# Spreading a group norm's factor over all partitions: two matmuls with a diagonal, or a round trip through DRAM on GpSimd's queue

## The chip, the cores and the metric

The kernel runs on one core of a Trainium2 chip. The metric is the device time of one execution in microseconds; the time before is the median of three runs. The profile is of one further execution. TensorE (PE) does matmuls, VectorE (DVE) and ScalarE (ACT) work on tiles in SBUF and PSUM, GpSimd (POOL) does small copies and products, and SyncE (SP) issues every transfer of the kernel before.

## The reference, cut to what matters

One step of a hybrid decoder layer. A prompt of 256 tokens with 16 learned tokens ahead of it, and 8 sample sequences of 8 tokens, go through an input projection, a Mamba-2 scan (64 heads in 8 groups), a short gated convolution, a merge of the two, and an output projection. The change touches the norm behind the scan:

```python
def gated_group_rms_norm(y, z, w):
    g = y.astype(jnp.float32) * jax.nn.silu(z.astype(jnp.float32))
    shp = g.shape
    g = g.reshape(shp[:-1] + (SSD_GROUPS, shp[-1] // SSD_GROUPS))
    g = g * lax.rsqrt(jnp.mean(g * g, axis=-1, keepdims=True) + EPS)
    return (g.reshape(shp) * w.astype(jnp.float32)).astype(y.dtype)
```

For each token and each of the 8 groups one factor, the inverse root of a mean over 512 channels, multiplies these 512 channels. All is float32; the kernel gets this accuracy by splitting each matmul operand into a rounded part and a rest (`hi`, `lo`).

## The kernel before, in words

All 336 tokens (320 are wanted in the end, `TV`) lie on the free axis and channels on the partitions. A weight tile of 128 outputs comes in two blocks of 128x1024 (`wblk`, L82 to L89): SP loads `wraw` (L84), ACT rounds it to `whi` (L86), DVE makes the rest `wlo` (L88). Each of the three tiles has three buffers. For each block TensorE multiplies eight pieces of `whi` with the rounded input and with its rest (L94, L95), then eight pieces of `wlo` with the rounded input (L98). So the `wlo` that DVE makes is read 16 matmuls after its `whi`. A projection unit (`unit`, `proj`) is two such blocks into one PSUM tile `pj`, of which there are two.

The scan is the function `ssd(g, st)`, a generator with `yield` between its steps, run for g = 0 to 7. `weave` (L677) runs the steps of `ssd(g)` between the projection units of the same stage: the gates `z_units(g)`, the output projection of the group before `out_units(g - 1)` (its inputs are `yh` and `yl`), and the convolution inputs of the next group `conv_units(g + 1)`; stage 7 has gate units in place of the last. Steps are spread evenly by matmul work. A scheduler then sets the order on each engine by times that it reckons for every instruction; each engine and SP's queue work in that fixed order.

At the end of `ssd(g)`:

- L602: three matmuls with a column of ones sum the squares, 107 tokens on partitions and 3 columns (321 = 320 tokens and a zero).
- L604 (DVE) scales and adds EPS, L605 (POOL) takes the power -0.5: `rs_r`, 107x3.
- L607 and L608 (DVE) split it into `rs_h`. L625 (DVE, twice) multiplies an identity with it: three diagonals side by side, 107x321, in a buffer called `xe`. L627 (TensorE, twice) multiplies ones with them, so that PSUM `ms` (`rs`) holds the 320 factors on each of the 128 partitions.
- L636 (DVE, four times) multiplies the four tiles `ys` by a weight and by `rs`, L637 (ACT) rounds to `yh`, L638 (DVE) makes the rest `yl`.
- Between these: L500/L502, the last product into the prompt's state `hst` (stored by L611, `ssmp`); L616/L619, the update of the sample states `h` in two halves of two tiles, stored by L629 (`ssms`); L519 loads the next group's `h` into the same four buffers.

In the same stretch, DVE runs `conv_tile` for the next group: three L398 on `cacc`, then L402 and L403 once ACT has done the tanh `cth` (L401). ACT fills `pad` (L389, L390) and the first product (L396); POOL copies three columns to and from `pad` (L391 to L393).

The names in rows: `pj<-hhi,wlo` is a tile written from tiles read; `W<-ac_d` broadcasts rows of a DRAM tensor to many partitions; `bq_d<-bhh` and `b<-bq_d` are another round trip through DRAM, on SP's queue.

Of the kernel before, what the change touches and what calls it, by code (L numbers as in the profile page):

```python
# [7 lines left out]
F32 = mybir.dt.float32  # L8
F32R = mybir.dt.float32r
# [4 lines left out]
P = 128  # L14
T = 336
META = 16
TV = T - META
# [13 lines left out]
V_CW, V_CB, V_NW, V_SNW, V_SCW, V_FW, V_D = 0, 192, 240, 256, 288, 336, 352  # L31
# [3 lines left out]
def fb(ap):  # L35
    return ap.bitcast(F32)


def bc(ap, shape):
    return ap.to_broadcast(shape)  # L40
# [3 lines left out]
def tile_hybrid_step(ctx, tc, xT, w1, w2, wdt, wso, wsc, wo, cmask, vec, hvec, convst, sconvst, h0T,  # L44
                     yT, convo, ssmp, ssms, sconvo):
    nc = tc.nc
    mult, add, sub = ALU.mult, ALU.add, ALU.subtract
# [3 lines left out]
    ps = ctx.enter_context(tc.tile_pool(name="ps", bufs=2, space=PSUM))  # L51
    dr = ctx.enter_context(tc.tile_pool(name="dr", bufs=1, space=bass.MemoryType.DRAM))
# [4 lines left out]
    xq_d = [dr.tile([80, 4, 512], F32, name=f"xq_d{i}") for i in range(2)]  # L57
    bq_d = [dr.tile([80, 4, P], F32, name=f"bq_d{i}") for i in range(2)]

    V = keep.tile([P, V_ALL], F32, name="V")  # L60
    CR = keep.tile([P, C_ALL], F32R, name="CR")
    HV = keep.tile([NH, 2], F32, name="HV")
# [6 lines left out]
    ident = CM[:, C_ID:C_ID + P]  # L69
    ones = CM[:, C_ONE:C_ONE + P]  # L70
    m1R, m1qR, onesR = CR[:, C_M1:C_M1 + P], CR[:80, C_M1Q:C_M1Q + 80], CR[:, C_ONE:C_ONE + P]
# [5 lines left out]
    def col(base, i):  # L77
        return V[:, base + i:base + i + 1]

    latest = {}  # L80

    def wblk(src, n=1024):  # L82
        raw = wp.tile([P, 1024], F32, name="wraw")
        nc.sync.dma_start(raw[:, :n], src)  # L84
        hi = wp.tile([P, 1024], F32R, name="whi")
        latest["act"] = nc.scalar.activation(hi[:, :n], raw[:, :n], AF.Copy).ins  # L86
        lo = wp.tile([P, 1024], F32R, name="wlo")
        latest["dve"] = nc.vector.tensor_tensor(lo[:, :n], raw[:, :n], fb(hi[:, :n]), sub).ins  # L88
        return hi, lo  # L89
# [20 lines left out]
    def rstd(pool, sums, t0, inv, eps):  # L110
        nt, w = T - t0, T // 3
        spans = [(a, a + w) for a in (0, w, nt - w)]
        pt_ = ps.tile([P, 512], F32, name="ms")
        for c, (a, b) in enumerate(spans):
            for i, sq in enumerate(sums):
                nc.tensor.matmul(pt_[:w, c:c + 1], sq[:, a:b], ones[:, 0:1],
                                 start=i == 0, stop=i == len(sums) - 1)
        m = pool.tile([P, 3], F32, name="rs_m", bufs=1)
        r = pool.tile([P, 3], F32, name="rs_r", bufs=1)
        nc.vector.tensor_scalar(m[:w], pt_[:w, 0:3], inv, eps, mult, add)  # L120
        nc.gpsimd.tensor_tensor(r[:w], m[:w], bc(mhalf[:w], [w, 3]), ALU.pow)
        yield
        pb_ = ps.tile([P, 512], F32, name="ms")
        for c, (a, b) in enumerate(spans):
            dg = pool.tile([P, P], F32, name="rs_d", tag="cbm", bufs=2)
            nc.vector.tensor_scalar(dg[:w, :w], ident[:w, :w], r[:w, c:c + 1], None, mult)
            nc.tensor.matmul(pb_[:, a:b], ones[:w, :], dg[:w, :w], start=True, stop=True)
        yield
        return pb_[:, :nt]

    def eights(ap, w=8):
        return ap.rearrange("p (b t) -> p b t", t=w)

    def run(gen):
        while True:
            try:
                next(gen)
            except StopIteration as e:
                return e.value
# [10 lines left out]
    with tc.tile_pool(name="pa", bufs=2) as pa:  # L150
        nc.sync.dma_start(V, vec)
        nc.sync.dma_start(ya[:, 0:2, :], xT[:, 0:2, :])
# [7 lines left out]
        wb[1].append(wblk(w2[32][:, 1024:2048]))  # L160
        nc.gpsimd.tensor_scalar(V[:, V_CW:V_CW + 240], V[:, V_CW:V_CW + 240], 0.5, None, mult)
        nc.gpsimd.tensor_scalar(V[:, V_SCW:V_SCW + 48], V[:, V_SCW:V_SCW + 48], 0.5, None, mult)
        uhi = pa.tile([P, KT, T], F32R, name="uhi", tag="vhi", bufs=1)
# [6 lines left out]
        for half in range(2):  # L170
            for k in range(8):
                for i in range(2):
                    hi, lo = wb[i][half]
                    kk = 8 * half + k
                    for j, (w, x) in enumerate(((hi, uhi), (hi, ulo), (lo, uhi))):
                        nc.tensor.matmul(pu[i][:, :T - 14], w[:, k * P:k * P + P], x[:, kk, 14:],
                                         start=kk == 0 and j == 0, stop=kk == 15 and j == 2)
# [4 lines left out]
        def conv_in(j, pr, pre=None, fac=None):  # L182
            c_s = pa.tile([P, T - 14], F32, name="c_s")
            if fac is None:
                nc.scalar.activation(c_s, pre[0] if pre else pr(w2[16 + j], 14), AF.Copy)
            else:
                nc.vector.tensor_tensor(c_s, pr(w2[16 + j], 14), fac, mult)
            ph = pre[1] if pre else pr(w2[32 + j], 14)
            up = pa.tile([P, 338], F32, name="up")
            ups = eights(up[:, 258:338], 10)  # L190
            nc.vector.tensor_tensor(up[:, :258], c_s[:, :258], ph[:, :258], mult)  # L191
            nc.vector.tensor_tensor(ups[:, :, 2:10], eights(c_s[:, 258:]), eights(ph[:, 258:]), mult)
            return up, ups
# [33 lines left out]
        rs = run(rstd(pa, [sacc], 0, 1.0 / DM, EPS))  # L227
# [25 lines left out]
        for j in range(KT):  # L253
            u = (up0, ups0) if j == 0 else u1 if j == 1 else conv_in(j, proj)
# [120 lines left out]
    with tc.tile_pool(name="pb", bufs=2) as pb:  # L375
# [62 lines left out]
        def big(tag, bufs, dt=F32):  # L438
            return pb.tile([P, 512], dt, name=tag, bufs=bufs)
# [4 lines left out]
        def ssd(g, st):  # L444
# [6 lines left out]
            W, xdt, xe, bt, cbm, hst = ([None] * 3 for _ in range(6))  # L451
# [3 lines left out]
            for c, w in enumerate(W):  # L455
                r = 80 if c == 2 else P
# [41 lines left out]
            def state(c, lhs, rhs):  # L498
                pst = ps.tile([P, 512], F32, name="ms") if c == 2 else ps.tile([P, 4, 512], F32, name="yb", bufs=1)[:, 0]
                nc.tensor.matmul(pst, lhs, rhs, start=True, stop=True)  # L500
                if c:
                    nc.vector.tensor_tensor(hst[c], hst[c], pst, add)  # L502
                else:
                    nc.scalar.activation(hst[c], pst, AF.Copy)
# [45 lines left out]
            for t in range(4):  # L550
                for i, (x, w, t0, n) in enumerate(((xdt[0], W[0], 0, P), (xdt[1], W[1], P, PX), (hst[0], E, P, PX),
                                                   (xdt[2][:80], W[2][:80], 272, 80))):
                    for q in range(2):
                        h = 2 * t + q
                        nc.tensor.matmul(yb[q * HP:(q + 1) * HP, t, t0:t0 + n], x[:, h * HP:(h + 1) * HP], w[:, h, :],  # L555
                                         start=i == 0, stop=i == 3)
# [46 lines left out]
            r = pb.tile([107, 3], F32, name="rs_r", bufs=1)  # L603
            nc.vector.tensor_scalar(r, pr[:107, 0:3], 1.0 / 512, 4.0 * EPS, mult, add)  # L604
            nc.gpsimd.tensor_tensor(r, r, bc(mhalf[:107], [107, 3]), ALU.pow)  # L605
            rh = pb.tile([107, 2, 3], F32R, name="rs_h", bufs=1)
            nc.vector.tensor_copy(rh[:, 0, :], r)  # L607
            nc.vector.tensor_tensor(rh[:, 1, :], r, fb(rh[:, 0, :]), sub)  # L608
            yield
            state(2, b3, x3)  # L610
            nc.sync.dma_start(ssmp[g], hst[2])  # L611
            for u in range(2):
                up = ps.tile([P, 4, 512], F32, name="yb", bufs=1)
                for b in range(4):
                    q = slice(32 * b, 32 * b + 32)
                    nc.tensor.matmul(up[:, b, :], bh[q, u, :], xh[q, u, :], start=True, stop=True)  # L616
                for b in range(2):
                    h = h0t[2 * u + b]
                    nc.vector.tensor_tensor(h, h, up[:, 2 * b:2 * b + 2, :], add)  # L619
                yield  # L620
                if u == 0:
                    rs = ps.tile([P, 512], F32, name="ms")
                    for i in range(2):
                        dg = big("xe", 2, F32R)[:107, :321]
                        nc.vector.tensor_tensor(eights(dg, 107), bc(ident[:107, :107].unsqueeze(1), [107, 3, 107]),  # L625
                                                bc(fb(rh[:, i, :]).unsqueeze(2), [107, 3, 107]), mult)
                        nc.tensor.matmul(rs[:, :TV], onesR[:107, :], dg[:, :TV], start=i == 0, stop=i == 1)  # L627
                for b in range(2):
                    nc.sync.dma_start(ssms[g, :, 4 * u + 2 * b:4 * u + 2 * b + 2, :], h0t[2 * u + b])  # L629
                yield  # L630
                if u == 0:
                    yh = pb.tile([P, 4, TV], F32R, name="yh", bufs=1)
                    yl = pb.tile([P, 4, TV], F32R, name="yl", bufs=1)
                    for t in range(4):
                        y = ys[:, t, META:]
                        nc.vector.scalar_tensor_tensor(y, y, col(V_SNW, 4 * g + t), rs[:, :TV], mult, mult)  # L636
                        nc.scalar.activation(yh[:, t, :], y, AF.Copy)  # L637
                        nc.vector.tensor_tensor(yl[:, t, :], y, fb(yh[:, t, :]), sub)  # L638
                    yield
# [81 lines left out]
    with tc.tile_pool(name="pc", bufs=3) as pc_:  # L721
# [12 lines left out]
        sm, r = (pc_.tile([107, 3], F32, name=n, bufs=1) for n in ("rs_m", "rs_r"))  # L734
# [18 lines left out]
        dg = pc_.tile([107, 3, 107], F32, name="rs_d", bufs=1)  # L753
        nc.vector.tensor_tensor(dg, bc(ident[:107, :107].unsqueeze(1), [107, 3, 107]),
                                bc(r.unsqueeze(2), [107, 3, 107]), mult)
        rs = ps.tile([P, 512], F32, name="pj")
# [111 lines left out]
```

## Time and profile before

| | |
|---|---|
| three runs | 1855.74, 1856.35, 1858.94 us; median 1856.35 |
| the profiled execution | 1857.97 us, of which the span from first to last instruction is 1856.0 |
| TensorE busy | 1828.3 us (99%), granted clock 0.995 |
| VectorE busy | 1133.9 us (61%) |
| ScalarE, GpSimd busy | 757.7 us (41%), 318.1 us (17%) |
| DMA | 53.8% of 16 engines' span, 179 GB/s, all from SP's queue but for instruction loads |
| the scan, stages 0 to 7 | the power of L605 at 840.5, 953.5, 1066.4, 1179.4, 1292.3, 1405.3, 1518.2 and 1625.6 us |

A stage takes 112.96 us, and the rows of one stage repeat in the next at that distance, but for stage 7. In the lists by time, the columns are: start in us, duration in us, engine, line, operation, tiles and shapes, count, and in brackets the idle time before it and what ended that. In the lists of transfers the last number is the median in us from issue to landing.

### The profile page before, as it was taken

What the parts mean: (1) busy time and instruction counts of PE and PEld (TensorE: products, weight loads), DVE (VectorE), ACT (ScalarE), POOL (GpSimd) and SP (SyncE); (2) the same over time, 40 slices, a digit from 0 to 9 for tenths busy, and PEclk for the clock granted to TensorE, in tenths of its full rate; (3) what the DMA queues carried; (4) which work ended last, traced back from release to release, by engine and by line L of the source; (5) the groups of instructions that cost most, each with busy time, mean ns of one, the idle gap of its engine ahead of it and who ended that gap; (6) DMA issues with size and microseconds to landing.
All of it is one profiled execution on the core that took longest, in us unless ns stands there. A gap on an engine that the chain in (4) does not pass through costs nothing.

```text
span 1856.0 us, 31512 instructions
## 1 busy us (share of the span) xinstructions
PE 1828.3 (99%) x12618; PEld 1792.8 (97%) x12618; DVE 1133.9 (61%) x1770; ACT 757.7 (41%) x1070; POOL 318.1 (17%) x411
## 2 busy tenths in 40 slices
PE   7999999999999999999999999999999999999996
PEld 7999999999999999999999999999999999999996
DVE  6844444454533335657577677876868777684533
ACT  6433333333333334534544353544535445333431
POOL 0100000000000001142142422314232142300111
PEclk9999999999999999999999999999999999999998
DMA  6444444444444446456466574655746566585553
GB/s 222 146 151 148 148 148 149 150 148 149 155 158 158 152 164 225 150 185 238 152 214 202 177 240 151 215 204 175 244 151 232 174 192 226 164 272 163 175 171 109
DMA packets 117186, 331.74 MB, mean 179 GB/s; under 512 B 12464, under 2 KB 38704, under 8 KB 117040
## 3 DMA queue, kind: packets, MB, share of 16 engines
q1 hardware_dynamic: 117040, 329.73, 53.8%
q8 instruction: 99, 1.62, 0.4%
q14 instruction: 47, 0.39, 0.1%
HBM read 296.80 MB, written 32.88 MB: 178 GB/s over the span
## 4 chain that ended last, share of the span: by engine, by line
PE 67%; DVE 1%; issue 1%; DMA 0%; ACT 0%; POOLq 0%; POOL 0%; DVEq 0%; ACTq 0%
PE pj L94 21%; PE pj L95 20%; PE pj L98 20%; PE yb L555 2%; PE ms L545 1%; PE yb L500 1%; PE ms L464 1%; DVE ya L761 0%; PE yb L616 0%; DVE wlo L88 0%; PE ms L467 0%; PE ms L559 0%; PE ms L602 0%; DMA h<-mb_d 0%; DMA wraw<-wso 0%
## 5 line engine op out<-in xcount | busy, mean ns | idle before, releaser
L94 PE MATMUL pj<-hhi,whi 128*128 128x320 f32 (+3 forms) x2944 | 886.6, 313 | 0.0
L95 PE MATMUL pj<-hlo,whi 128*128 128x320 f32 (+3 forms) x2944 | 882.2, 312 | 0.0
L88 DVE TENSOR_TENSOR wlo<-wraw,whi 128x1024 fp32r<-128x1024 f32 x480 | 596.7, 1243 | 462.0 <-PE pj L98 235.8
L86 ACT ACTIVATE whi<-wraw 128x1024 fp32r<-128x1024 f32 x480 | 508.7, 1060 | 861.8 <-PE pj L95 746.0
L94 PEld LDWEIGHTS pj<-hhi,whi 128*128 128x128 f32 x2944 | 553.8, 188 | 4.1 <-ACT yh L637 1.7
L95 PEld LDWEIGHTS pj<-hlo,whi 128*128 128x128 f32 x2944 | 553.0, 188 | 0.3 <-issue 0.2
L98 PE MATMUL pj<-hhi,wlo 128*128 128x320 f32 (+3 forms) x2944 | 498.4, 311 | 0.0
L98 PEld LDWEIGHTS pj<-hhi,wlo 128*128 128x128 f32 x2944 | 453.2, 188 | 0.0
L94 PE MATMUL pj<-yh,whi 128*128 128x320 f32 x512 | 156.2, 317 | 1.8 <-ACT zs L433 1.1
L95 PE MATMUL pj<-yl,whi 128*128 128x320 f32 x512 | 152.2, 309 | 0.0
L508 POOL TENSOR_TENSOR h<-h,decS 128x512 f32<-128x512 f32 x64 | 72.4, 1164 | 185.8 <-PE ms L545 185.8
L94 PEld LDWEIGHTS pj<-yh,whi 128*128 128x128 f32 x512 | 96.2, 188 | 4.8 <-issue 2.2
L95 PEld LDWEIGHTS pj<-yl,whi 128*128 128x128 f32 x512 | 96.3, 188 | 1.7 <-issue 1.7
L98 PE MATMUL pj<-yh,wlo 128*128 128x320 f32 x512 | 95.9, 309 | 0.0
L398 DVE SCALAR_TENSOR_TENSOR cacc<-pad,V,cacc 128x360 f32<-128x360 f32 (+1 forms) x144 | 89.5, 622 | 2.2
L654 DVE TENSOR_TENSOR ya<-ya,pj 128x320 f32<-128x320 f32 x112 | 54.2, 485 | 57.3 <-PE pj L98 56.5
L197 POOL COPY SCS<-up 128x2 f32<-128x2 f32 x16 | 19.4, 1215 | 369.8 <-DVE up L191 366.7
L98 PEld LDWEIGHTS pj<-yh,wlo 128*128 128x128 f32 x512 | 80.4, 188 | 0.0
L95 PE MATMUL pj<-vlo,whi 128*128 128x320 f32 x256 | 75.5, 309 | 0.0
L94 PE MATMUL pj<-vhi,whi 128*128 128x320 f32 x256 | 75.5, 309 | 0.0
L392 POOL COPY cs<-pad 128x3 f32<-128x3 f32 x48 | 41.9, 873 | 81.2 <-ACT pad L389 80.6
L391 POOL COPY pad<-cs 128x24 f32<-128x24 f32 x48 | 33.6, 702 | 114.3 <-DVE cacc L398 93.0
(225 smaller groups left out, 1491.6 us busy)
## 6 DMA issues: line engine op xcount, KB each, us to landing
wraw<-w SPq DMA_DIRECT2D x352, 512.0 KB, 3.9
wraw<-wso SPq DMA_DIRECT2D x64, 512.0 KB, 3.6
wraw<-wsc SPq DMA_DIRECT2D x32, 512.0 KB, 3.8
h<-h0T SPq DMA_DIRECT2D x32, 512.0 KB, 5.6
ssms<-h SPq DMA_DIRECT2D x32, 512.0 KB, 5.3
wraw<-wo SPq DMA_DIRECT2D x32, 512.0 KB, 3.7
xq_d<-xe SPq DMA_DIRECT2D x16, 320.0 KB, 3.4
W<-ac_d SPq DMA_DIRECT2D x8, 576.0 KB, 6.1
```

What stands on the lines that cost most here:

```text
L86: latest["act"] = nc.scalar.activation(hi[:, :n], raw[:, :n], AF.Copy).ins
L88: latest["dve"] = nc.vector.tensor_tensor(lo[:, :n], raw[:, :n], fb(hi[:, :n]), sub).ins
L94: nc.tensor.matmul(out, w, xh(k0 + k), start=first and k == 0, stop=False)
L95: nc.tensor.matmul(out, w, xl(k0 + k), start=False, stop=False)
L98: latest["pe"] = nc.tensor.matmul(out, w, xh(k0 + k), start=False, stop=last and k == nk - 1).ins
L197: nc.gpsimd.tensor_copy(SCS[:, j, 0, :], up[:, 256:258])
L391: nc.gpsimd.tensor_copy(smp[:, :, 0:3], cs[:, 1:9, :])
L392: nc.gpsimd.tensor_copy(cs[:, 0, :], pad[:, 272:275])
L398: nc.vector.scalar_tensor_tensor(acc[:, i0:], pad[:, i0 + k:360 + k], col(V_CW, 4 * j + k), acc[:, i0:], mult, add)
L508: nc.gpsimd.tensor_tensor(split(h0[b]), split(h0[b]), bc(hv(decS[:, b, :], g), [P, 8, HP]), mult)
L555: nc.tensor.matmul(yb[q * HP:(q + 1) * HP, t, t0:t0 + n], x[:, h * HP:(h + 1) * HP], w[:, h, :], start=i == 0, stop=i == 3)
L654: nc.vector.tensor_tensor(ya[:, m, :TV], ya[:, m, :TV], pp[:, :TV], add)
```

## The change

The factor `rs_r` no longer goes through the two diagonals and matmuls. GpSimd stores it to a DRAM tensor `r_d` of 321 values (two of them, by turns), in an order that puts the token index in line, and in the next step loads the 320 values from there to all 128 partitions, into a buffer of `xe` in SBUF. Both transfers are issued on POOL. L636 reads the factor from there, no longer from PSUM. L607, L608, L625 and L627 go.

```diff
+    r_d = [dr.tile([321], F32, name=f"r_d{i}") for i in range(2)]
...
             nc.gpsimd.tensor_tensor(r, r, bc(mhalf[:107], [107, 3]), ALU.pow)
-            rh = pb.tile([107, 2, 3], F32R, name="rs_h", bufs=1)
-            nc.vector.tensor_copy(rh[:, 0, :], r)
-            nc.vector.tensor_tensor(rh[:, 1, :], r, fb(rh[:, 0, :]), sub)
-            yield
+            nc.gpsimd.dma_start(r_d[g % 2].rearrange("(c p) -> p c", p=107), r)
+            yield
+            rs = big("xe", 2)[:, :TV]
+            nc.gpsimd.dma_start(rs, r_d[g % 2][:TV].partition_broadcast(P))
             state(2, b3, x3)
...
                 yield
-                if u == 0:
-                    rs = ps.tile([P, 512], F32, name="ms")
-                    for i in range(2):
-                        dg = big("xe", 2, F32R)[:107, :321]
-                        nc.vector.tensor_tensor(eights(dg, 107), bc(ident[:107, :107].unsqueeze(1), [107, 3, 107]),
-                                                bc(fb(rh[:, i, :]).unsqueeze(2), [107, 3, 107]), mult)
-                        nc.tensor.matmul(rs[:, :TV], onesR[:107, :], dg[:, :TV], start=i == 0, stop=i == 1)
                 for b in range(2):
...
-                        nc.vector.scalar_tensor_tensor(y, y, col(V_SNW, 4 * g + t), rs[:, :TV], mult, mult)
+                        nc.vector.scalar_tensor_tensor(y, y, col(V_SNW, 4 * g + t), rs, mult, mult)
```

The scheduler sets the order anew. Line numbers after are one higher up to L620 and six lower behind that: L88 is L89, L398 is L399, L502 is L503, L519 is L520, L619 is L620, L629 is L623, L636 is L630, L638 is L632.

On VectorE, stage 0, before, these rows follow the convolution's L403; the first of the four multiplications by the factor (L636) is the last of them:

```order
462 L403 SCALAR_TENSOR_TENSOR xs<-cth,cacc 128x64
463 L625 TENSOR_TENSOR xe<-CR,rs_h 107x321 x2
464 L88 TENSOR_TENSOR wlo<-wraw,whi 128x1024
465 L502 TENSOR_TENSOR hst<-hst,ms 128x512
466 L398 SCALAR_TENSOR_TENSOR cacc<-pad_6678,V,cacc 128x360
467 L619 TENSOR_TENSOR h_7387<-h_7387,yb 128x1024
468 L398 SCALAR_TENSOR_TENSOR cacc<-pad_6678,V,cacc 128x360
...
475 L636 SCALAR_TENSOR_TENSOR ys<-ys,V,ms 128x320
```

and after:

```order
458 L404 SCALAR_TENSOR_TENSOR xs<-cth,cacc 128x64
459 L630 SCALAR_TENSOR_TENSOR ys<-ys,V,xe 128x320 x3
460 L503 TENSOR_TENSOR hst<-hst,ms 128x512
461 L632 TENSOR_TENSOR yl<-ys,yh 128x320
462 L620 TENSOR_TENSOR h_7389<-h_7389,yb 128x1024
463 L399 SCALAR_TENSOR_TENSOR cacc<-pad_6680,V,cacc 128x360
464 L620 TENSOR_TENSOR h_7391<-h_7391,yb 128x1024
...
469 L630 SCALAR_TENSOR_TENSOR ys<-ys,V,xe 128x320
470 L403 SCALAR_TENSOR_TENSOR xs<-cth,cacc 128x272
471 L404 SCALAR_TENSOR_TENSOR xs<-cth,cacc 128x64
472 L89 TENSOR_TENSOR wlo<-wraw,whi 128x1024
```

The multiplications by the factor moved up by a dozen rows, to right behind the convolution's L403, and the `wlo` that stood there (row 464 before) now stands behind them, the state update and most of the `yl` (row 472 after).

On POOL, in the same place, after:

```order
112 L607 DMA r_d_75<-rs_r 107x3x1
113 L392 COPY pad_6679<-cs 128x8x3
114 L610 DMA xe<-r_d_75 128x320
115 L590 MEMSET b_9254 64x128
116 L393 COPY cs<-pad_6680 128x3
```

The store and the load are new; between them stands one copy that was there before, and behind the load, which waits for the store to have landed, stand the clearing of `b` and the next copies for `pad`.

On SP's queue, before:

```order
127 L84 DMA wraw<-w 128x1024 x6
128 L611 DMA ssmp<-hst 128x512
129 L629 DMA ssms<-h_7387 128x1024
130 L629 DMA ssms<-h_7389 128x1024
131 L84 DMA wraw<-w 128x1024
132 L519 DMA h_8624<-h0T 128x1024
133 L84 DMA wraw<-w 128x1024
```

and after:

```order
127 L85 DMA wraw<-w 128x1024 x5
128 L612 DMA ssmp<-hst 128x512
129 L623 DMA ssms<-h_7389 128x1024
130 L623 DMA ssms<-h_7391 128x1024
131 L520 DMA h_8619<-h0T 128x1024
132 L520 DMA h_8621<-h0T 128x1024
133 L85 DMA wraw<-w 128x1024 x4
```

One load of weights fewer stands ahead of the three stores, and both loads of `h` now stand ahead of the next weights.

## The prediction

> **What bounds the kernel now.** I read the page's engine lines first, then the chain that ended last, then the busy time in the stretch of the change.
>
> ```profile
> span 1856.0 us, 31512 instructions
> PE 1828.3 (99%) x12618; PEld 1792.8 (97%) x12618; DVE 1133.9 (61%) x1770; ACT 757.7 (41%) x1070; POOL 318.1 (17%) x411
> PE 67%; DVE 1%; issue 1%; DMA 0%; ACT 0%; POOLq 0%; POOL 0%; DVEq 0%; ACTq 0%
> 836.00:870.00 34.00, 34.00 (x226) 33.01 (x225) 28.35 (x49) 17.13 (x29) 8.75 (x16) 1.00 0.64 218
> ```
>
> The first two lines give the bound: TensorE works through the whole span. The chain (third) names no other engine above 1%. In the stretch from 836 to 870 us, which holds the end of stage 0 of the scan, TensorE is busy for 34.00 of 34.00 us at full clock and VectorE for 28.35. So a step gains only what it takes off TensorE, and costs only when something reaches TensorE late. VectorE has 5.6 us of air in 34: the place to look for lateness.
>
> **What goes.** TensorE, by time, around the two spreading matmuls of stage 0:
>
> ```profile
> 853.90 1.40 PE L98 MATMUL pj<-hhi,wlo 128*128 128x336 f32 x8
> 855.13 0.46 PE L627 MATMUL ms<-xe,CR 107*128 107x320 f32 x2
> 855.43 0.32 PE L94 MATMUL pj<-hhi,whi 128*128 128x336 f32 x1
> 857.91 1.40 PE L98 MATMUL pj<-hhi,wlo 128*128 128x336 f32 x8
> 867.01 0.31 PE L94 MATMUL pj<-hhi,whi 128*128 128x320 f32 x1
> 1637.72 1.34 PE L98 MATMUL pj<-hhi,wlo 128*128 128x320 f32 x8
> ```
>
> From the start of L627 to the start of what follows is 855.43 - 855.13 = 0.30 us, with no wait in it. Eight stages: 2.4 us come off the bound engine. That is the whole gain that I can see. The VectorE instructions that go (two small ones and the diagonals, 1.2 us a stage) lie beside TensorE's work and are worth nothing while the weights are on time.
>
> **What comes.** POOL's rows of the same place, and the same instruction in the last two stages:
>
> ```profile
> 840.49 0.87 POOL L605 TENSOR_TENSOR rs_r<-rs_r,mhalf 107x3 f32<-107x3 f32 x1
> 842.82 0.21 POOL L391 COPY pad<-cs 128x24 f32<-128x24 f32 x1 [1.46 <-DVE cacc L398]
> 852.83 1.56 POOL L391 COPY pad<-cs 128x24 f32<-128x24 f32 x1 [4.31 <-DVE cacc L398]
> 1518.23 0.87 POOL L605 TENSOR_TENSOR rs_r<-rs_r,mhalf 107x3 f32<-107x3 f32 x1
> 1625.62 0.86 POOL L605 TENSOR_TENSOR rs_r<-rs_r,mhalf 107x3 f32<-107x3 f32 x1 [12.48 <-DVE rs_r L604]
> ```
>
> The factor is ready at 840.49 + 0.87 = 841.36. Then come the store to DRAM, the wait for its landing on POOL, and the load to 128 partitions. Call the time of this chain D; the factor is in SBUF at R = 841.36 + D. Stages 0 to 6 repeat at 112.96 us ((1518.23 - 840.49)/6), so one working serves seven.
>
> POOL itself: behind the waiting load stand the clearing of `b` and the `pad` copies. The copy at 842.82 is ahead of the wait; the next `pad` copy starts only at 852.83. A store that lands within 10 us delays none that counts.
>
> VectorE is where the wait matters, because its queue now has three multiplications by the factor right behind L403, and the weights' rest `wlo` that stood there stands a dozen instructions later. Rows of before that give each step:
>
> ```profile
> 843.40 1.23 DVE L88 TENSOR_TENSOR wlo<-wraw,whi 128x1024 fp32r<-128x1024 f32 x1 [0.70 <-PE pj L98]
> 844.54 0.43 DVE L402 SCALAR_TENSOR_TENSOR xs<-cth,cacc 128x272 f32<-128x272 f32 x1
> 844.89 0.22 DVE L403 SCALAR_TENSOR_TENSOR xs<-cth,cacc 128x64 f32<-128x64 f32 x1
> 845.03 0.89 DVE L625 TENSOR_TENSOR xe<-CR,rs_h 107x321 fp32r<-107x321 f32 x2
> 847.11 1.23 DVE L88 TENSOR_TENSOR wlo<-wraw,whi 128x1024 fp32r<-128x1024 f32 x1 [1.19 <-ACT whi L86]
> 848.25 0.68 DVE L502 TENSOR_TENSOR hst<-hst,ms 128x512 f32<-128x512 f32 x1
> 848.85 0.59 DVE L398 SCALAR_TENSOR_TENSOR cacc<-pad,V,cacc 128x360 f32<-128x360 f32 x1
> 849.35 1.22 DVE L619 TENSOR_TENSOR h<-h,yb 128x1024 f32<-128x1024 f32 x1
> 850.48 0.59 DVE L398 SCALAR_TENSOR_TENSOR cacc<-pad,V,cacc 128x360 f32<-128x360 f32 x1
> 856.53 0.54 DVE L636 SCALAR_TENSOR_TENSOR ys<-ys,V,ms 128x320 f32<-128x320 f32 x1
> 856.99 0.59 DVE L398 SCALAR_TENSOR_TENSOR cacc<-pad,V,cacc 128x360 f32<-128x360 f32 x1
> 858.46 0.48 DVE L638 TENSOR_TENSOR yl<-ys,yh 128x320 fp32r<-128x320 f32 x1
> 858.86 0.58 DVE L398 SCALAR_TENSOR_TENSOR cacc<-pad,V,cacc 128x360 f32<-128x360 f32 x1
> ```
>
> VectorE arrives at the first multiplication at 845.03, where L625 began. If D is under 3.7 it never waits. Otherwise it starts at R, and by the distance from start to start runs: three multiplications 3 x 0.46, L502 0.60, one rest 0.40, L619 1.13, L398 0.50, L619 1.13, L398 0.50, rest 0.40, L398 0.50, rest 0.40, the fourth multiplication 0.46, L402 0.35, L403 0.14, and L88 itself 1.23: 9.12. The `wlo` is done at R + 9.12. ScalarE's parts between (rounding, tanh) are half a microsecond each and have a place before they are asked for.
>
> When does TensorE read it? The `wlo` at 843.40 waited for TensorE to end the block whose L98 ended about 843.1; with three buffers it belongs to the third block after that one. The block of 847.11 is one later, and its L98 starts at 857.91; without L627 that is 857.6, and the weight load is some 0.1 ahead. So R + 9.12 must not pass 857.5: R up to 848.4, D up to 7.0 us. Beyond that each microsecond of D is one of TensorE's, in seven stages. In the last stage the order is another: behind R stand three multiplications, a rest, the fourth and a `wlo` (1.38 + 0.40 + 0.46 + 1.23 = 3.5), read at 1637.72 - 0.3 = 1637.4; the factor's power ends at 1626.48, so there D may be 7.4.
>
> What else is behind: SP's queue now loads weights only after both stores of `h` are issued and have landed and the next `h` is loaded.
>
> ```profile
> ssms<-h SPq DMA_DIRECT2D x32, 512.0 KB, 5.3
> h<-h0T SPq DMA_DIRECT2D x32, 512.0 KB, 5.6
> wraw<-w SPq DMA_DIRECT2D x352, 512.0 KB, 3.9
> SPq L519 <- DMA ssms<-h: 33.0, 19, 3.7
> ```
>
> The fourth line shows that this wait exists already. The second store can go at R + 5.2 (after both L619), lands at R + 10.5; a load of `h` and then of weights are issued by R + 11.2 and land 3.9 to 5.6 later; rounding takes 1.1: `whi` at R + 16.2 to 17.9. These are the weights of the block that TensorE starts at 867.01, now 866.7. D may be 7.4 to 9.1: the first limit comes earlier, and a stall there pushes this one back. I cost it at nothing.
>
> **How long is D?** No transfer of the trace is issued by POOL, and none writes single elements, so I bound both legs by rows of SP's queue.
>
> ```profile
> ac_d<-acx SPq DMA_DIRECT2D x1, 4.0 KB, 4.4
> W<-ac_d SPq DMA_DIRECT2D x8, 200.0 KB, 2.9
> DMA to landing us min/median/max: 1.7/2.5/4.4
> DMA to landing us min/median/max: 2.1/3.0/3.9
> DMA to landing us min/median/max: 3.4/3.9/5.4
> DMA to landing us min/median/max: 2.5/5.5/6.3
> ```
>
> The last four are the stores of `sg_d` (L666), the loads of `b` from DRAM, the stores of `bq_d` (L577) and the broadcasts of `W` (L457). Shortest: a store of 1.7 and a load of 2.1, D = 3.8. Longest: 5.4 and 6.3, D = 11.7. The nearest row for the store is `acx`, 64 short pieces into DRAM apart from each other (4.4); for the load the broadcast of 200 KB (2.9), the nearest in size to our 160 KB. With 0.1 for each of two hand-overs on POOL, as between L604 and L605, D = 7.5. Stall: (7.5 - 7.0) x 7 + (7.5 - 7.4) = 3.6 us.
>
> The sum: -2.4 + 3.6 = +1.2 us on the profiled execution, 1857.97 to 1859.2. That execution was 1.6 above the median of 1856.35 (its span alone is 1856.0), so as a median I say 1857.6. About 0.2%, 3.7 us, is what a measurement of this kernel can tell from no change.
>
> For the legs' price there is a figure: the Trainium skill, DMA: Bandwidth & Descriptors, section on the anatomy of a DMA on the gpsimd path, fits about 2.0 us plus bytes over 436 GB/s to each DMA issued from GpSimd. By that D would be an estimated 2.0 + 2.0 + 0.4 = 4.4, under the limit, and the sum -2.4. No row here shows it; SP's rows lie above it under this kernel's traffic.
>
> **Rivals.** *Hidden.* D stays under 7.0 and the factor costs nothing: 1856.35 - 2.4 = 1854.0. For it: the shortest legs (3.8) and half of the rows in between; VectorE even gets shorter. Against it: 321 pieces of four bytes, where the shortest rows move long ones.
>
> *Slower, the load on the 16 engines.* D between 7.8 and 11.9 (the longest rows and the hand-overs): 1860 to (4.9 x 7 + 4.5 - 2.4 = 36) 1893. For it: the stretch moves 218 GB/s, and `wraw`, `hst` and `h` go out in it. Against it: the medians, 3.9 and 3.0.
>
> *Slower, the pieces in single file.* The store's 321 pieces (each value goes to an address of its own) are worked off by one DMA engine and not by 16. The broadcast of 200 KB has 640 pieces, 40 for each engine; taken at 2.9 - 1.7 = 1.2 us above the shortest landing, 0.03 us a piece. 321 of them in file: 9.6 us. D = 1.7 + 9.6 + 2.9 + 0.2 = 14.4, stall 7.4 x 7 + 7.0 = 58.8, 1912.8; it decides from about 100 pieces in one file on (3.0 us, D = 7.8). For it: 107 partitions cannot be dealt out evenly over 16. Against it: the store of 80 partitions in the trace shows no such length, but 80 can be. The Trainium skill, DMA: Bandwidth & Descriptors, section on why a DMA increments its semaphore by 16, has such a rule: the number of engines is the largest up to 16 that divides the slowest dimension on both sides, which for 107 is one; it also names an exception, measured for some direct copies on GpSimd's path, where uneven partitions are spread all the same. No run here shows which holds.
>
> That the change does not do what it says is excluded by the order of instructions: 16 matmuls are gone from TensorE's.
>
> **How the numbers follow.** The forecast, D up to 7.8, so that the factor lands about when it is wanted: 1853.9 to 1860, chance 0.5, of which 0.2 is the hidden case. Load on the engines, 1860 to 1893: 0.28. Single file, about 1913 and up: 0.2. A gain over 3.7 us has no source in the trace: 0.02. So faster 0.02, same 0.5, slower 0.48. The range of 1853.5 to 1890 leaves out the single file and little else.
>
> **What would show it.** TensorE without L627 at 99%; POOL's queue with a wait of some 4 us for the store in each stage; VectorE waiting at the first L630 for the load, R - 845.0, 3.8 us by my D; TensorE's weight loads at L98 waiting for `wlo` by up to half a microsecond in seven stages. I am wrong if VectorE waits over 4.5 us there (then TensorE waits visibly, once a stage) or not at all. The store's landing decides: 4.4 is my figure, and one of 10 or more would mean single file. Also wrong would be a TensorE wait for `whi` behind late `wraw`, which I cost at nothing.

## The result, and the profile after

| | before | after |
|---|---|---|
| median of four runs each | 1857.01 us | 1983.64 us (1981.79 to 1988.80) |
| ratio | | 1.0686, 95% interval 1.0672 to 1.0700 |
| profiled execution, its span | 1857.97, 1856.0 us | 1988.80, 1986.7 us |

The kernel became 6.9% slower, where I had forecast no change and a range up to 1890. From the page of the changed kernel: the span, the engines, the chain by engine; and from its list of transfers the two new ones, with their median from issue to landing.

```profile
span 1986.7 us, 31494 instructions
PE 1864.0 (94%) x12602; PEld 1824.2 (92%) x12602; DVE 1120.2 (56%) x1738; ACT 748.9 (38%) x1070; POOL 346.1 (17%) x427
PE 55%; DMA 8%; DVE 5%; issue 1%; POOL 1%; ACT 0%; POOLq 0%; DVEq 0%; ACTq 0%
```

```profile
xe<-r_d POOLq DMA_DIRECT2D x8, 160.0 KB, 4.3
r_d<-rs_r POOLq DMA_DIRECT2D x8, 1.3 KB, 15.0
```

TensorE is no longer busy all the time (94% after 99%), and the chain now has 8% of DMA, which it had not. The load took 4.3 us; the store, which I had put at 4.4, took 15.0. The chain in order of time, in stage 0 (start, duration):

```profile
843.73 14.77 DMA r_d<-rs_r
858.54 0.52 issue
859.08 4.15 DMA xe<-r_d
863.25 1.48 DVE ys L630 x3
```

The power ends at 843.42, so D is 863.25 - 843.42 = 19.8 us and not 7.5. Where the store's 14.8 us go is seen on GpSimd, in the busy times by stretch (length, then PE, PEld, DVE, ACT, POOL, then granted clock, share of the 16 DMA engines, GB/s), and in the share of GpSimd's own queue (`q0`: packets, MB, share of the 16 engines) from 850 to 854:

```profile
843.73 4.01 POOL L607 DMA_DIRECT2D r_d<-rs_r  x1 [0.31 <-POOL rs_r L606]
```

```profile
850.00:851.00 1.00, 1.00 (x8) 1.00 (x7) 0.00 (x0) 0.00 (x0) 0.00 (x0) 1.00 0.95 15
854.00:856.00 2.00, 2.00 (x15) 2.00 (x14) 0.00 (x0) 0.00 (x0) 0.00 (x0) 1.00 0.00 0
856.00:858.50 2.50, 1.35 (x9) 1.07 (x7) 0.00 (x0) 0.00 (x0) 0.00 (x0) 1.00 0.00 0
```

```profile
q0 software_dynamic: 85, 0.01, 59.2%
```

GpSimd needs 4.0 us to issue it. Then the 16 engines are 95% busy at 15 GB/s, and 59% of them from 850 to 854 is GpSimd's queue with 0.01 MB: they work on the store. From 854 on nothing moves, yet the landing is reported only at 858.5. So it is 4 us of issue, some 5.5 of movement, 5 of silence. VectorE and ScalarE stand still from 850 on (0.00). What the engines waited for, in the whole run (us in total, times, longest):

```profile
DVE ys L630 <- DMA xe<-r_d: 136.1, 8, 20.9
ACT yh L631 <- DVE ys L630: 132.3, 15, 22.9
PE pj L95 <- ACT pad L391: 54.4, 7, 8.9
PE pj L99 <- DVE wlo L89: 21.6, 7, 3.4
PE pj L95 <- ACT cacc L658: 14.0, 1, 14.0
```

The waits of TensorE come to 90 us and explain most of the loss. The rest is in TensorE's own rows of stage 0:

```profile
855.95 1.40 PE L99 MATMUL pj<-hhi,wlo 128*128 128x336 f32 x8
864.76 0.65 PE L95 MATMUL pj<-hhi,whi 128*128 128x336 f32 x1 [7.41 <-ACT pad L391]
868.57 0.45 PE L96 MATMUL pj<-hlo,whi 128*128 128x336 f32 x1
868.85 0.32 PE L95 MATMUL pj<-hhi,whi 128*128 128x336 f32 x1
869.01 0.32 PE L96 MATMUL pj<-hlo,whi 128*128 128x336 f32 x1
872.44 1.77 PE L99 MATMUL pj<-hhi,wlo 128*128 128x336 f32 x5 [3.11 <-DVE wlo L89]
```

```profile
866.00:868.00 2.00, 2.00 (x8) 2.00 (x8) 2.00 (x3) 0.95 (x1) 0.00 (x0) 0.50 0.50 193
```

After the pause of 7.4 us the matmuls follow each other at 0.28 us instead of 0.155, for 3.8 us; the granted clock there is 0.50. So this wait costs twice, once as idle time and again as slow matmuls; TensorE's busy time rose from 1828.3 to 1864.0 with fewer matmuls. The Trainium skill, TensorE: Matmul & The Clock Gate, Part 1 (what's actually happening), says that an idle window of about 3.4 us puts the array's clock to half, and that it takes about as long of busy time to get it back; this trace agrees (0.50, 3.8 us).

### The profile page after: what moved, and what is told of

Its sections match the earlier page's. It is cut to its first block, busy times and chain, and to the rows that moved or that the text cites. A ratio compares the mean times of both kernels' runs of the same rounds, so it can differ in the third digit from the quotient of the medians.

```text
span 1986.7 us, 31494 instructions
## 1 busy us (share of the span) xinstructions
PE 1864.0 (94%) x12602; PEld 1824.2 (92%) x12602; DVE 1120.2 (56%) x1738; ACT 748.9 (38%) x1070; POOL 346.1 (17%) x427
## 4 chain that ended last, share of the span: by engine, by line
PE 55%; DMA 8%; DVE 5%; issue 1%; POOL 1%; ACT 0%; POOLq 0%; DVEq 0%; ACTq 0%
PE pj L99 17%; PE pj L95 17%; PE pj L96 17%; DMA r_d<-rs_r 6%; DMA xe<-r_d 2%; PE yb L556 1%; DVE h L620 1%; DVE wlo L89 1%; DVE ys L630 1%; PE ms L546 1%; PE yb L501 1%; DVE cacc L399 1%; PE ms L465 0%; DVE yl L632 0%; DVE ya L755 0%
## 5 line engine op out<-in xcount | busy, mean ns | idle before, releaser
L95 PE MATMUL pj<-hhi,whi 128*128 128x320 f32 (+3 forms) x2944 | 901.5, 317 | 54.4 <-ACT pad L391 54.4
L96 PE MATMUL pj<-hlo,whi 128*128 128x320 f32 (+3 forms) x2944 | 895.0, 316 | 0.0
L89 DVE TENSOR_TENSOR wlo<-wraw,whi 128x1024 fp32r<-128x1024 f32 x480 | 596.1, 1244 | 466.4 <-PE pj L99 236.1
L95 PEld LDWEIGHTS pj<-hhi,whi 128*128 128x128 f32 x2944 | 565.8, 192 | 60.5 <-ACT pad L391 56.4
L96 PEld LDWEIGHTS pj<-hlo,whi 128*128 128x128 f32 x2944 | 564.5, 192 | 0.3 <-issue 0.2
L99 PE MATMUL pj<-hhi,wlo 128*128 128x320 f32 (+3 forms) x2944 | 505.9, 314 | 21.6 <-DVE wlo L89 21.6
L99 PEld LDWEIGHTS pj<-hhi,wlo 128*128 128x128 f32 x2944 | 458.8, 190 | 23.9 <-DVE wlo L89 23.9
L630 DVE SCALAR_TENSOR_TENSOR ys<-ys,V,xe 128x320 f32<-128x320 f32 x32 | 16.1, 546 | 136.1 <-DMA xe<-r_d 136.1
L399 DVE SCALAR_TENSOR_TENSOR cacc<-pad,V,cacc 128x360 f32<-128x360 f32 (+1 forms) x144 | 89.5, 622 | 3.2
L393 POOL COPY cs<-pad 128x3 f32<-128x3 f32 x48 | 50.9, 1059 | 120.3 <-ACT pad L390 85.1
```

Source lines behind the costliest of these rows:

```text
L95: nc.tensor.matmul(out, w, xh(k0 + k), start=first and k == 0, stop=False)
L96: nc.tensor.matmul(out, w, xl(k0 + k), start=False, stop=False)
L99: latest["pe"] = nc.tensor.matmul(out, w, xh(k0 + k), start=False, stop=last and k == nk - 1).ins
L393: nc.gpsimd.tensor_copy(cs[:, 0, :], pad[:, 272:275])
L399: nc.vector.scalar_tensor_tensor(acc[:, i0:], pad[:, i0 + k:360 + k], col(V_CW, 4 * j + k), acc[:, i0:], mult, add)
```

## The experiments

In each kernel below, one stage is measured by the starts of the first and the last power, seven stages apart: 785.1 us before (840.5 to 1625.6), 893.0 after. "Early" and "late" are the two places of the multiplications (L630).

**What makes the store long.** My theories were the number of pieces (A), the 107 partitions (B, the single file of the prediction) and GpSimd's queue (C). Three kernels change the pieces and the partitions.

107 pieces of 12 bytes:

```diff
-                nc.tensor.matmul(pr[:107, c:c + 1], zs[0][:, 107 * c:107 * c + 107], ...)
+                nc.tensor.matmul(pr[:107, c:c + 1], zs[0][:, c:321:3], ...)
...
-            nc.gpsimd.dma_start(r_d[g % 2].rearrange("(c p) -> p c", p=107), r)
+            nc.gpsimd.dma_start(r_d[g % 2].rearrange("(p c) -> p c", c=3), r)
```

> The changed kernel, with the columns of the three sums taken three apart, so that each of the 107 partitions holds three neighbouring tokens: the store goes out as 107 pieces of 12 bytes instead of 321 of 4. In the changed kernel the factor came 19.8 us after the power's end (D) and the kernel lost 16.1 us a stage, 1.26 us for each us of D above 7.0; so I read the time as 1854 + 10.1 x (D - 7.0). Theory A (the cost goes with the number of pieces): issue about 1.5 us instead of 3.9, landing 5 to 8 us instead of 15.0, D 10 to 13, time 1885 to 1915. Theory B (107 partitions cannot be dealt out over 16 engines, the pieces go in single file): a third of the pieces, but still one file; landing 9 or 10, D about 14, time about 1925. Theory C (GpSimd's own queue is slow whatever it carries): landing stays at 13 to 15, time 1960 or more.

80 partitions, 320 single values:

```diff
+            for c in range(4):
+                nc.tensor.matmul(pr[:80, c:c + 1], zs[0][:, 80 * c:80 * c + 80], ...)
...
+            nc.gpsimd.dma_start(r_d[g % 2][:TV].rearrange("(c p) -> p c", p=80), r)
```

> The changed kernel with the factor held as 80 partitions x 4 instead of 107 x 3: 320 pieces of 4 bytes go out as before, but 80 can be dealt out evenly over 16 engines. Theory A (number of pieces): nothing changes, landing about 15, time 1975 to 1990. Theory B (107 is the culprit, single file): landing about 4 to 6, D 9 to 11, time 1875 to 1895. Theory C (the queue): as the changed kernel, about 1984.

80 partitions, 80 pieces of 16 bytes:

```diff
+                nc.tensor.matmul(pr[:80, c:c + 1], zs[0][:, c:320:4], ...)
...
+            nc.gpsimd.dma_start(r_d[g % 2][:TV].rearrange("(p c) -> p c", c=4), r)
```

> 80 partitions x 4 neighbouring tokens: the store goes out as 80 pieces of 16 bytes, dealt evenly over 16 engines. Theory A (number of pieces): a quarter of them; issue about 1 us, landing 4 to 6, D 9 to 11, time 1875 to 1895. Theory B (single file because of 107): the same or less, about 1875, so this run does not tell A from B by itself, but with the two others it does. Theory C (the queue): landing 13 or more, time 1960 or more.

Measured: 1895.12, 1944.49 and 1883.23 us, ratios to before 1.0198 (1.0181 to 1.0215), 1.0465 (1.0442 to 1.0488) and 1.0139 (1.0106 to 1.0171). The store's issue on GpSimd (ns, minimum/median/maximum) and its landing, in this order:

```profile
L607 POOL DMA_DIRECT2D r_d<-rs_r x8: 652/654/793, 843.0 to 1656.9; - x8
DMA to landing us min/median/max: 2.9/3.0/8.4
```

```profile
L607 POOL DMA_DIRECT2D r_d<-rs_r x8: 722/726/867, 843.2 to 1705.9; - x8
DMA to landing us min/median/max: 8.9/9.3/12.5
```

```profile
L607 POOL DMA_DIRECT2D r_d<-rs_r x8: 610/610/760, 844.9 to 1652.9; - x8
DMA to landing us min/median/max: 2.3/2.4/7.3
```

The times of the first and the third lie in A's ranges, but by luck in part: their landings are below A's (3.0 against 5 to 8, 2.4 against 4 to 6), and I had put a wait of a given length too cheap. The second fits neither A nor B.

With whole rows the landing is 2.4 for 80 partitions and 3.0 for 107: GpSimd's queue is not slow in itself, so C falls. With single values it is 9.3 for 80: the pieces cost 6.9 us at the same partitions, so B is not the whole either. Single values from 107 partitions cost another 5.7 (15.0), of which 3.1 are GpSimd's issue (3.85 against 0.73). A is the main cause, the combination adds to it, and why it does is open; on GpSimd's queue it is not one engine that carries the store (59% of 16 in the changed kernel, above). How the pieces cost their time is open too: with 320 single values, in stage 0, all packets of GpSimd's queue fall before 845.4, within 2.2 us of the start of the issue at 843.2, and the landing comes at 852.8. The Trainium skill, DMA: Bandwidth & Descriptors, section on why a DMA increments its semaphore by 16, gives 107 partitions to one engine and names an exception for some direct copies on GpSimd's path, which spread them. The trace of the changed kernel agrees with the exception (the 59%).

**The same store on another queue.** ScalarE issues the 321 values:

```diff
-            nc.gpsimd.dma_start(r_d[g % 2].rearrange("(c p) -> p c", p=107), r)
+            nc.scalar.dma_start(r_d[g % 2].rearrange("(c p) -> p c", p=107), r)
```

> The changed kernel with the same 321 single values, stored by ScalarE's queue instead of GpSimd's; the load stays on GpSimd. ScalarE waits for the power about 1 us. Theory A (the pieces cost, whoever issues them; GpSimd's own preparation of 3.9 us is a part of it that falls away): landing 8 to 11 us, D about 13 to 15, time 1915 to 1945. Rival (GpSimd's path makes it slow, the pieces do not): landing 3 to 5, D 7 to 9.5, time 1880 to 1898.

1969.05 us, ratio 1.0602 (1.0587 to 1.0616). The store in the chain, in stage 1 and in the last, and the share of ScalarE's queue (`q10`) from 968 to 979 us:

```profile
967.48 12.19 DMA r_d<-rs_r
1718.99 19.92 DMA r_d<-rs_r
```

```profile
q10 hardware_dynamic: 322, 0.00, 6.7%
```

In stages 0 to 6 the store takes 11.1 to 12.2 us without GpSimd's preparation, of 15 with it: the single values are slow whoever issues them. But they go another way. 6.7% of 16 engines is 1.07 engines: the 322 packets keep about as much as one engine busy for the whole 11 us, as the single file of theory B would. The view does not name the engines. My time for A was too low by 24 us, since D was 17, not 13 to 15 (the load landed 4.8 after its issue, and GpSimd issued it late).

**The transfers without the wait.** The kernel before keeps its matmuls; the store runs beside it, and a load to a tile that nothing reads.

```diff
+            nc.gpsimd.dma_start(r_d[g % 2].rearrange("(c p) -> p c", p=107), r)
             yield
+            sp_ = pb.tile([P, 112], F32, name="spare", bufs=1)
+            nc.gpsimd.dma_start(sp_, r_d[g % 2][:112].partition_broadcast(P))
```

> The kernel before, with its two spreading matmuls, and beside them the same store of 321 single values on GpSimd's queue and a load of 112 of them to a spare tile that nothing reads. It carries the transfers and POOL's wait, but VectorE waits for none of it. Theory A (the loss is the wait for the factor): 1856 +- 4. Rival (the loss is the load that 321 small pieces put on the DMA engines, or POOL's late pad copies): at least a third of the loss appears, 1895 or more; TensorE would wait for ScalarE's or POOL's pad or for late weights.

The second one stores 107 rows of 12 bytes, `"(p c) -> p c", c=3`, with all else the same:

> The kernel before with its matmuls, and beside them a store of the factor as 107 pieces of 12 bytes and the load to a spare tile that nothing reads (the order in DRAM is not the tokens' order, and nothing uses it). The same with 321 single values took 1869, 11.5 us over the kernel before. Theory A (the single values hold up weight loads on the DMA engines): with 107 pieces the extra is gone, 1856 to 1860. Rival (any transfer of GpSimd's there costs, by POOL's wait or by its queue): 1866 to 1871 again.

Single values: 1869.36 us, ratio 1.0062 (1.0041 to 1.0084). Rows: 1858.24, ratio 1.0003 (0.9994 to 1.0012). So 11.5 of the 126.6 us lost can come from the small pieces as a load on the DMA engines, without anyone waiting for the factor; the rest needs the wait. Neither theory had this size. Where it comes from, in the kernel with single values: a load of weights that meets the store (issued at 1635.0), and ScalarE behind it.

```profile
1639.00 14.48 DMA wraw<-wso
```

```profile
1653.59 1.06 ACT L87 ACTIVATE whi<-wraw 128x1024 fp32r<-128x1024 f32 x1 [9.16 <-DMA wraw<-wso]
```

14.5 us instead of the median of 3.5 of these loads. In most stages the stretch has room for it (112.97 to 113.2 us between powers); one stage (117.15), with a load of weights of 11.8 us in its chain (at 1196.0), and the last had not.

**What the wait costs.** Multiplications one step later, with the store of the changed kernel and with 80 rows of 16 bytes:

```diff
-                if u == 0:
+                if u == 1:
                     yh = pb.tile([P, 4, TV], F32R, name="yh", bufs=1)
```

> The changed kernel, its 321 single values as they are, with the multiplications one step later. D stays 20; VectorE arrives at 13 and waits some 7 us a stage instead of 16 to 17. Theory A (each us of VectorE's wait is about 0.9 us of TensorE's, as the four runs with the multiplications early show: 2.9, 4.0, 10.9 and 14.9 us a stage at D of 7.2, 9.1, 15.6 and 20.3): 6 us a stage, 1895 to 1915. Rival (the small pieces on the DMA engines cost by themselves): a higher time than that, 1930 or more. Second rival (7 us of wait can be made up later in the stage, since the state's update now stands ahead of it): 1856 to 1875.

> The kernel with 80 pieces of 16 bytes (factor in SBUF 7.2 us after the power's end, D), and the block of the four multiplications by the factor one step later in the program (behind the second half's stores of h instead of the first's). VectorE then reaches the first multiplication some 13 us after the power's end, where the kernel before reached it at 15.2. Theory A (what costs is only VectorE's wait at a place where it comes too early): no wait at the multiplication, the 2.4 us of the removed matmuls show, 1852 to 1857. Rival (the round trip costs by its transfers, or by SP's stores and loads of h standing ahead of the weights): 1865 to 1880, with TensorE waiting for cbm or wlo as in the run with 80 pieces of 16 bytes.

321 values, late: 1944.82 us, ratio 1.0464 (1.0447 to 1.0480). Its waits and those of the kernel with 80 rows, late:

```profile
DVE ys L630 <- DMA xe<-r_d: 92.5, 8, 19.2
```

```profile
DVE ys L630 <- DMA xe<-r_d: 9.1, 1, 9.1
```

The first was a miss in size: D grew to 22.3 to 25.3 (the store landed after 17.8, as it does in the kernel where nobody waits for it), so VectorE waited 10.5 us a stage and not 7, and nothing of it was made up. With 80 rows VectorE does not wait in stages 0 to 6 at all. It took 1865.71, ratio 1.0038 (1.0025 to 1.0051), against 1852 to 1857 expected. The 8 us have two causes. One is the last stage, where the store lands after 7.6 and VectorE waits 9.1: from the last power to the end of the span it is 237.5 us, and 230.4 before. The other is the sums with ones, which I had changed along with the store: TensorE's row for them in the kernel before, with three columns taken three apart, and with four taken four apart:

```profile
1177.74 0.63 PE L602 MATMUL ms<-CR,zs 128*107 128x1 f32 x6
```

```profile
1190.06 0.90 PE L603 MATMUL ms<-CR,zs 128*107 128x1 f32 x6
```

```profile
1187.74 1.19 PE L603 MATMUL ms<-CR,zs 128*80 128x1 f32 x8
```

On the bound engine that is 0.27 and 0.56 us a stage, about what the removed matmuls had given, and nearly twice that. With it taken out, the kernels with a wait in every stage stand on one line, per stage of 0 to 6:

| kernel | VectorE's wait for the factor | stage longer by | of that TensorE's own work | remainder |
|---|---|---|---|---|
| 80 rows, early | 3.3 | 3.3 | +0.3 | 3.0 |
| 107 rows, early | 5.0 | 4.1 | 0.0 | 4.1 |
| 321 values, late | 10.5 | 10.1 | -0.3 | 10.4 |
| 320 values, early | 11.9 | 11.1 | -0.3 | 11.3 |
| 321 values by ScalarE | 13.6 | 13.3 | -0.3 | 13.6 |
| 321 values (the change) | 16.5 | 15.4 | -0.3 | 15.7 |

(The wait is the total less the last stage's, by seven: (136.1 - 20.9)/7 = 16.5. The stage: (893.0 - 785.1)/7 = 15.4.) Each microsecond that VectorE waits is one of the stage's, less 0 to 1 us. I had given it 3.3 us of room. The rows point to about no loss at no wait, so the new order by itself costs little; no run has the early place without a wait.

**Who hands it on.** In the kernel with 80 rows, early, the wait is within the room that I had reckoned, and the `wlo` that I had followed is indeed on time (first row); TensorE waits elsewhere, 2 us a stage:

```profile
PE pj L99 <- DVE wlo L89: 0.5, 2, 0.3
PE ms L467 <- DVE cbm L475: 14.2, 7, 3.0
```

From the chain of that kernel in stage 1, some 10 to 40 us behind the first multiplication (967.4):

```profile
978.11 5.65 DMA wraw<-w
986.16 1.13 DVE h L620
987.80 1.14 DVE h L620
988.96 6.66 DMA ssms<-h
996.10 7.19 DMA wraw<-w
1003.37 1.07 ACT whi L87
1004.46 0.85 DVE wlo L89
```

It starts with a load of weights, which waited for VectorE's `wlo` to free a buffer (976.91 to 978.1). From there it runs through the second half's `h`, their stores, SP's queue (the loads of the next `h` and then weights behind these stores) to a late `wlo`, behind which `cbm` stands on VectorE. The stretch over SP's queue was the edge that I had costed at nothing. To take it away, I moved the stores of the states and the loads of `h` from SP's queue to GpSimd's, in the kernel with 107 rows, early:

```diff
-                nc.sync.dma_start(h, h0T[g, :, 2 * u:2 * u + 2, :])
+                nc.gpsimd.dma_start(h, h0T[g, :, 2 * u:2 * u + 2, :])
...
-            nc.sync.dma_start(ssmp[g], hst[2])
+            nc.gpsimd.dma_start(ssmp[g], hst[2])
...
-                    nc.sync.dma_start(ssms[g, ...], h0t[2 * u + b])
+                    nc.gpsimd.dma_start(ssms[g, ...], h0t[2 * u + b])
```

> The kernel with 107 pieces of 12 bytes (multiplications early, VectorE waits 5 us a stage, 1895), with the stores of the states and the loads of the next h issued by GpSimd instead of SP, so that SP's queue holds the weights alone there. Theory A (what makes VectorE's wait cost from the first microsecond is SP's queue: weights stand behind the stores and loads of h, which stand behind the multiplications): most of the 4.2 us a stage goes, 1860 to 1875. Rival (VectorE's own queue is late for the whole stage, whatever the weights do): 1890 to 1900. GpSimd now waits for these stores before some pad copies; if that is what then bounds, TensorE waits for ScalarE's cacc or VectorE's xs, and the time is 1890 or more with another wait.

1897.56 us, ratio 1.0223 (1.0208 to 1.0239); it had been 1895.12. Nothing was won: VectorE waits 4.9 us a stage and the stage is 4.3 longer, as in the table. So SP's order alone is not the carrier, and the time is that of the rival, a VectorE that is late for the whole stage. The chain, and the wait of SP's queue for a buffer of weights:

```profile
988.21 1.15 DVE wlo L89
989.37 8.09 DMA wraw<-w
997.54 1.07 ACT whi L87
998.63 0.85 DVE wlo L89
```

```profile
SPq L85 <- DVE wlo L89: 1206.5, 418, 14.5
```

Now the weights are late because their buffer comes free late: SP waits for VectorE's `wlo`, and the load then takes 8 us. The sum of these waits shows little, for it is 1088.6 us in the kernel before and 1055.3 ahead of the move, where SP waited at the stores of `h` instead; the longest grew from 9.1 to 14.5. In both kernels the late thing is weights, once through the queue and the buffers and once through the buffers alone that a late VectorE holds. GpSimd's transfers of `h` share the engines with that load, which this run does not separate. That the buffers are the last link in general I have not shown.

**A version that keeps the gain.** Stages 0 to 6 late with 107 rows, stage 7 as before:

```diff
+            last = g == NG - 1
...
-                if u == 0:
+                if u == (0 if last else 1):
                     yh = pb.tile([P, 4, TV], F32R, name="yh", bufs=1)
```

> In stages 0 to 6 the round trip with 107 pieces of 12 bytes and the multiplications one step later; in stage 7 the two diagonals and matmuls of the kernel before. Three column sums as before, not four (with 80 x 4 the eight matmuls of the sums took 1.05 us of TensorE against 0.49). If the wait and the small pieces were all that cost, VectorE reaches the multiplication at 13.3 us, the factor is there at 9, and a stage takes 112.96 - 0.30 = 112.66 us: 2.1 us less in all, 1854 to 1856. Rival (the late order costs something of its own, as the 8 us of the late run with 80 pieces may say): 1858 to 1866, with stages of 112.9 or more.

The next one takes 80 neighbouring columns four times, stores 80 rows of 16 bytes, and lets VectorE read the transposed factor:

```diff
-                            nc.vector.scalar_tensor_tensor(y, y, col(V_SNW, 4 * g + t), rs, mult, mult)
+                            yv = y.rearrange("q (c p) -> q c p", p=80)
+                            nc.vector.scalar_tensor_tensor(yv, yv, col(V_SNW, 4 * g + t), rs.rearrange("q (p c) -> q c p", c=4), mult, mult)
```

> As the run before last (round trip one step later in stages 0 to 6, matmuls in stage 7), but with 80 x 4 columns taken in one piece each, stored as 80 rows of 16 bytes; the order in DRAM is then transposed, and VectorE reads the factor with a stride of 16 bytes. TensorE's sums with columns taken three apart took 0.76 us against 0.49; with 80 neighbouring columns 0.53. A stage should take 112.96 - 0.30 + 0.04 = 112.70, seven stages 1.8 us less: 1855.5 against 1857.4, a ratio of 0.9990. Rival: the strided read makes the multiplications longer (over 0.6 us each against 0.54), but VectorE has the room, so the time does not change for it; if it does, stages of 112.9 or more.

With 107 rows: 1856.31 us, ratio 0.9995 (0.9987 to 1.0004), no difference; I had expected 1854 to 1856, without the sums, which cost 0.27 of the 0.30. With 80 rows: 1854.60 against 1856.86, ratio 0.9986 (0.9977 to 0.9995). The stores of stages 0 and 6 in the two, and the multiplications of the second:

```profile
L613 POOL DMA_DIRECT2D r_d<-rs_r x7: 652/657/793, 843.6 to 1521.1; - x7
```

```profile
L614 POOL DMA_DIRECT2D r_d<-rs_r x7: 610/610/760, 842.4 to 1518.5; - x7
```

```profile
L649 DVE SCALAR_TENSOR_TENSOR ys<-ys,V,xe 128x320 f32<-128x320 f32 x28 | 21.3, 804 | 0.0
```

A stage takes (1521.1 - 843.6)/6 = 112.92 and 112.68 us, against 112.96 before and 112.70 expected for the second. The strided multiplication takes 804 ns instead of 546, which VectorE has room for. So the idea is worth 0.3 us a stage at most, and it is to be had only where nobody waits for the round trip.

## Why the prediction was wrong

- *What bounds the kernel, and what goes*: right. Where nothing waits, a stage gets shorter by the 0.30 us of L627 (112.68, with 0.04 more for the sums).
- *D*: this step failed. I bounded the store by 1.7 to 5.4 us, from rows of SP's queue, and took 4.4 from 64 short pieces as the nearest; it measured 15.0. I noted that no row writes single values, and still let rows of longer pieces set the upper end. The load was sized well enough (2.9, measured 4.3); the two hand-overs, 0.1 each in my sum, took 0.3 and 0.6. A D of 20.2 (mean of stages 0 to 6; 24.3 in the last) in place of 7.5 is the bulk: by my own formula (20.2 - 7.0) x 7 + (24.3 - 7.4) - 2.4 = 107 us, of the 131 by which the two spans differ.
- *The limit of 7.0*: the second failure, some 20 us. It holds for the one `wlo` that I followed (0.5 us of waiting in all at D = 7.2), but the room of 3.3 us in front of it is not room for the stage: of 3.3 us waited, 3.0 were lost. The edge over SP's queue, which I "cost at nothing" because the first limit came earlier, is the chain in that kernel, and with SP's queue freed of `h` the weights are late all the same.
- *ScalarE's parts "have a place before they are asked for"*: wrong at this D. They stand in order behind the rounding of the product, `yh`, which waits for VectorE (132.3 us), and TensorE waited longest for the `pad` behind it (54.4 us).
- *TensorE at half clock after a pause* was not in the sum.
- *POOL*: I called a landing within 10 us harmless; it came after 15, and no wait of TensorE names a copy of POOL's.
- *The rivals.* The single file came nearest with 1912.8 and up, and I gave it 0.2. Its sign was right, a store of over 10 us because of its pieces, but on GpSimd's queue not its mechanism: more than one engine works on the store (59% of 16), and 80 partitions are slow too. That its time is the nearest is in part luck. On ScalarE's queue the store behaves as this rival says, down to its length: 11.1 to 12.2 us, against 1.7 + 9.6 = 11.3. The load on the engines was put at the wrong transfer: it is this store that delays weights (14.5 us), worth 11.5 us by itself.
- *The estimate of 4.4 for both legs.* The Trainium skill's fit of about 2.0 us plus bytes over 436 GB/s for a DMA from GpSimd (DMA: Bandwidth & Descriptors, anatomy of a DMA on the gpsimd path) is near what rows of 16 bytes took (2.4) and far from single values (15.0). I had written that SP's rows lie above it, but the shortest two make 3.8 for both legs.

## What to carry to other kernels

The price of this store went by how many separate pieces it writes, not by its bytes: from 107 partitions 1.3 KB took 15.0 us as 321 values and 3.0 as rows, from 80 partitions 9.3 and 2.4, while the load of 160 KB took 4.3. So choose the layout so that a partition's values are neighbours in DRAM, and where the profile has no row of such pieces, leave the upper bound open. If the consumer stands in an in-order queue, place it behind the whole round trip (13 us here) rather than reckon with slack behind it: here each microsecond waited was nearly one lost. Look also at what the new layout does to the bound engine's reads: columns taken three or four apart ate the gain.

## What I had not expected of the hardware

- GpSimd needed 3.85 us to issue a store of 321 single values from 107 partitions, and 0.73 us for 320 single values from 80.
- After the last movement on the DMA engines the landing of that store was reported some 5 us later (853.5 to 858.5). The Trainium skill, DMA: Bandwidth & Descriptors, anatomy of a DMA on the gpsimd path, says that the semaphore waits until the last write is confirmed and that this can be surprisingly long when the target is HBM; no run here shows what the time is spent on.
- The small pieces hold up others: beside the unread store two loads of 512 KB of weights took 14.5 and 11.8 us, where the medians of their kinds are 3.5 and 3.7.
- The same 321 values kept more than one engine busy from GpSimd's queue (59% of 16, 850 to 854 us) and about one from ScalarE's (6.7% of 16).
- Matmuls whose stationary operand is read with a stride of three columns were dearer: the row of the sums grew from 0.63 to 0.90 us.
